# Order of TensorE's products with stationary weight columns: blocks of eight and eight in place of two and two

## The chip, the cores and the metric

The kernel runs on one core of one Trainium2 chip. The metric is the device time of one execution in microseconds (us), smaller is better. Engines are called as in the profile: PE is TensorE (PEld its weight loads), ACT is ScalarE, DVE is VectorE, POOL is GpSimd, SP is SyncE.

## The reference

A decoder trunk of four layers over 256 tokens and 2048 features, in float32. Layers 0 and 3 use latent attention, layer 1 sparse attention, layer 2 sliding-window attention. Each layer is one block:

```python
h = rmsnorm(x, norm_in[i])
self_out, mq, gate = mixer(h, ...)             # one projection makes q/k/v or latents, mq and gate
mem_out = memory_attention(mq, mem_n @ w_mem_kv[i])
y = concatenate([self_out, mem_out], -1) * silu(gate)
x = x + y @ w_out[i]
```

and a last rmsnorm ends it. Most of the work is products of 256 rows with weight matrices that come from HBM (511.62 MB are moved in all).

## The kernel before

**Two parts for each number.** The products keep nearly float32 accuracy with operands of type fp32r. Each operand is split into a high part, its rounded copy, and a low part, what is left. `split` (L67 to L69) makes the high part on ACT (`copy_act`, L60) and the low part on DVE as a subtraction (L69). A product is then high × high + high × low + low × high.

**Two ways of multiplying.** `rows_by` (L240) holds feature columns stationary in PE and streams weights past them, up to 512 columns: three products for each half of the rows and each feature tile of 128 (L265, L266, L267). `columns_by` (L270), which is changed here, holds weight columns stationary and streams the features, so its result stands transposed. It makes 256 output columns in two halves j of 128. For each feature tile kt of 128 and each half it has

- one product of 512 columns (L285): the high weight part `wh` stationary, and streaming past it both parts of the features, 256 columns each, side by side; the accumulator `acc[j]` keeps the two results apart in one PSUM bank,
- one product of 256 columns (L289): the low weight part `wl` stationary, and the high features streaming; it is added to the first half of `acc[j]`.

Each product has a weight load of its own (128 × 128). The order written in the code is, for each feature tile: two products of 512 (j = 0, 1), then two of 256 (j = 0, 1). Four feature tiles make a block: one weight load from HBM by `stage` (L217, issued by SP into one of five `wr` buffers of 512 KB), one call of `other_work`, and two calls of `parts_of`, each of which splits the weights of two feature tiles, a `wh` and a `wl` of 128 × 512. There are three buffers for `wh` and three for `wl`.

`columns_by` serves the keys of the memory (`mk`, L432), the gates (`g`, L462), the memory queries (`mq`, L548) and, in the latent layers, the compressed queries (`cq`, L641), the queries (`qn`, L688) and the keys (`kn`, L693). It has 16, 12 or 4 feature tiles, always whole blocks. The results are combined by `total` (ACT and DVE) or by `head_parts`.

**What sets the order.** The program is written as straight code, and a scheduler of the framework gives each engine a fixed order, from the order of the code, a simulated timeline and the free buffers. Products of attention (L487 transposes, L565 and L586 memory attention, L719, L921, L924 scores, L455 transposes) get places among the projections. At run time each engine goes through its own order and waits at semaphores. Only a few instructions, mostly DMAs, are pinned to the order of the code.

Of the kernel before, what the change touches and what calls it, by code (L numbers as in the profile page):

```python
# [15 lines left out]
P = 128  # L16
S = 256
# [14 lines left out]
def kernel(ctx: ExitStack, tc: tile.TileContext, a: dict, out: bass.AP,  # L32
                             kinds=(0, 1, 2, 0)):
    nc = tc.nc
# [32 lines left out]
    def split(hi, lo, src):  # L67
        copy_act(hi, src)
        nc.vector.tensor_sub(lo, src, f32(hi))  # L69
# [136 lines left out]
    def stage(w, k0, m, cols, each=None):  # L206

        n = cols[1] if len(cols) == 2 else cols[1] * cols[4]
        wr = wp.tile([P, ST * 512], F32, name="wr", tag="wr", bufs=WR)
        src = w[k0 * P:(k0 + m) * P, :].rearrange("(k p) n -> p k n", p=P)  # L210
        dst = wr[:, :m * n].rearrange("p (k n) -> p k n", k=m)
        if each is not None:
            for k in range(m):
                tc.keep_in_program_order(nc.sync.dma_start(dst[:, k, :], src[:, k, cols[0]:cols[0] + n]))
                each(k0 + k)
        elif len(cols) == 2:
            nc.sync.dma_start(dst, src[:, :, cols[0]:cols[0] + n])  # L217
        else:
            c0, r, step, off, width = cols
            for k in range(m):  # L220
                nc.sync.dma_start(dst[:, k, :].rearrange("p (r c) -> p r c", r=r),
                                  src[:, k, c0:c0 + r * step].rearrange("p (r c) -> p r c", r=r)
                                  [:, :, off:off + width])
        return wr, n
# [4 lines left out]
    def other_work():  # L229
        for _ in range(2):  # L230
            if steps and next(steps[0], None) is None:
                steps.pop(0)

    def parts_of(wr, c0, n):
        wh = wp.tile([P, 512], F32R, name="wh", tag="wh", bufs=3)
        wl = wp.tile([P, 512], F32R, name="wl", tag="wl", bufs=3)
        split(wh[:, :n], wl[:, :n], wr[:, c0:c0 + n])
        return wh, wl
# [31 lines left out]
    def columns_by(xt, kts, w, k0, cols, name):  # L270

        acc = [ps.tile([P, 2, S], F32, name=f"acc_{name}{j}", tag="acc", bufs=4) for j in range(2)]
        for s in range(0, kts, 2 * ST):
            m = min(2 * ST, kts - s)
            wr, n = stage(w, k0 + s, m, cols)
            other_work()
            for k2 in range(0, m, 2):
                wh, wl = parts_of(wr, k2 * S, 2 * S)
                for k in range(2):
                    kt = s + k2 + k  # L280
                    q = xt[kt // 4]

                    for j in range(2):
                        o = k * S + j * P
                        nc.tensor.matmul(acc[j], wh[:, o:o + P], q[:, :, kt % 4, :],  # L285
                                         start=kt == 0, stop=False)
                    for j in range(2):
                        o = k * S + j * P
                        nc.tensor.matmul(acc[j][:, 0, :], wl[:, o:o + P], q[:, 0, kt % 4, :],  # L289
                                         start=False, stop=kt == kts - 1)  # L290
        return acc

    def total(acc, name="z"):
# [70 lines left out]
    def memory():  # L364
# [54 lines left out]
        for i in range(depth):  # L419
            w = a["w_mem_kv"][i]  # L420
            for p_ in range(2):
                begins = i == p_ == 0
                if begins:

                    pinned.append(0)
                    acc = rows_by(mT, 16, w, 0, (MEMW, 512), "mv", prepare, each)
                    pinned.pop()
                    mrow = [memory_rows(c) for c in range(4)]
                else:
                    values(i, p_, rows_by(mT, 16, w, 0, (MEMW + p_ * 512, 512), "mv"))  # L430
                for h in (2 * p_, 2 * p_ + 1):
                    acck = columns_by(mT, 16, w, 0, (h * 256, 256), "mk")  # L432
                    if begins and h == 0:
                        row_scales(mrow)
                        values(i, p_, acc)
                    keys(i, h, acck)
                step = 2 * i + p_
                if begins:

                    not_before(f32(mT[3])[:, 0, 3, :1])  # L440
                    late_constants()
                    bias_table(0)
                    bias_table(1)
                if 1 <= step < 5:
                    steps.append(nm.first_chunk(step - 1))
# [13 lines left out]
    def gate(nm, w, c0):  # L459
        gT = act.tile([P, 4, S], F32, name="gT", tag="gT", bufs=2)  # L460
        for h in range(2):
            acc = columns_by(nm.at, 16, w, 0, (c0 + h * S, S), "g")  # L462
            for j in range(2):
                z = total(acc[j])
                hz = wk.tile([P, S], F32, name="hz", tag="z", bufs=3)
                nc.vector.tensor_mul(hz, z, nm.half)
                th = wk.tile([P, S], F32, name="th", tag="e", bufs=4)
                nc.scalar.activation(th, hz, AF.Tanh)
                nc.vector.scalar_tensor_tensor(gT[:, 2 * h + j, :], th, 1.0, hz, op0=OP.add, op1=OP.mult)
        return gT  # L470
# [65 lines left out]
    def memory_project(nm, i, w, mq0, g0, part, behind):  # L536
        kT, qT = [], []
        if part == 0:
            not_before(behind)
        v = [act.tile([P, 2, 512], F32R, name="mvr", tag="aux", bufs=AUX) for z in range(2)]  # L540
        pin = tc.keep_in_program_order if part == 0 else lambda inst: inst
        for z in range(2):
            pin(nc.gpsimd.dma_start(v[z], mv[i][part][:, z]))
        for h in range(2):
            k = act.tile([P, 2, 2, S], F32R, name="mkr", tag="pq", bufs=PQ)
            pin(nc.gpsimd.dma_start(k, mkT[i][2 * part + h]))
            kT.append(k)
            acc = columns_by(nm.at, 16, w, 0, (mq0 + part * 512 + h * 256, 256), "mq")  # L548
            q = act.tile([P, 2, 2, S], F32R, name="mqT", tag="pq", bufs=PQ)
            head_parts(q, acc)  # L550
            qT.append(q)
        return nm, kT, v, qT, gate(nm, w, g0 + 2048 + part * 512)
# [538 lines left out]
```

## Time and profile before

| | |
|---|---|
| median of 3 runs | 2592.52 us (2592.51 to 2592.64) |
| the profiled execution | 2594.19 us |
| its span, first to last instruction | 2592.4 us |
| mean granted TensorE clock | 0.998 |
| ACT waiting for PE's products of L285 with `acc_g`, before `wh` | 175.5 us in 254 waits |

The profile is of one execution. A row of the groups gives line, engine, operation, output <- inputs, shape and count, then the busy time in us and the mean ns of one, then the idle time of the engine just before. In the timeline a row gives the start in us, the length in us, engine, line, operation and count; neighbours of one kind are merged to one row, which runs from the start of the first to the end of the last. Products overlap: one starts while the one before it still drains, so the distance between starts is shorter than the length of one. A row of the waits says who waited for whom, the total in us, how often, and the longest.

### The profile page before, as it was taken

Reading aid. Unit: us, or ns where it says so; the run is one execution under the profiler, and the core shown is the slowest. Engines: PE = TensorE matmul, PEld = TensorE weight load, DVE = VectorE, ACT = ScalarE, POOL = GpSimd, SP = SyncE. Lnnn points to the kernel's source line nnn. Section 1 sums busy time; section 2 is a strip of 40 time slices with the busy share of each in tenths; the row PEclk is TensorE's granted clock in tenths of the full one; section 3 lists DMA queues with packets and bytes.
Section 4 is the critical chain, followed back from the end, with each engine's and each line's share of the span. In section 5 each row is a group of like instructions: output and inputs, shape, how many; then the busy total and the mean of one; then the engine's idle time right before and its main releaser. Section 6 shows DMA issues by size and latency. Waiting matters only on the chain.

```text
span 2592.4 us, 41637 instructions
## 1 busy us (share of the span) xinstructions
PE 2574.6 (99%) x14038; PEld 2213.6 (85%) x14038; DVE 1875.6 (72%) x4126; ACT 1619.6 (62%) x3435; POOL 67.3 (3%) x123
## 2 busy tenths in 40 slices
PE   9999999999999999999999999999999999999998
PEld 7888898888888888888888888888889888888886
DVE  6666667667776686877778776777778767676667
ACT  6555556556656566667666666676666655665655
POOL 1000000000000010000000000000000000000000
PEclk9999999999999999999999999999999999999999
DMA  9887777666676667566556575555655766566764
GB/s 302 255 256 257 242 214 234 184 171 190 193 202 201 199 215 249 165 202 191 184 170 197 170 226 168 176 172 184 195 157 152 231 185 166 170 168 182 212 178 132
DMA packets 456279, 511.62 MB, mean 197 GB/s; under 512 B 68944, under 2 KB 351840, under 8 KB 454912
## 3 DMA queue, kind: packets, MB, share of 16 engines
q1 hardware_dynamic: 442544, 451.68, 58.3%
q0 software_dynamic: 13088, 56.16, 6.8%
q8 instruction: 110, 1.80, 0.3%
q10 hardware_dynamic: 432, 1.11, 0.1%
q14 instruction: 105, 0.86, 0.1%
HBM read 489.91 MB, written 31.56 MB: 201 GB/s over the span
## 4 chain that ended last, share of the span: by engine, by line
PE 91%; DVE 0%; ACT 0%; issue 0%; ACTq 0%
PE acc_g L285 14%; PE acc_g L289 7%; PE acc_wo L265 7%; PE acc_wo L266 7%; PE acc_wo L267 7%; PE acc_mq L285 5%; PE acc_cq L285 3%; PE acc_qn L285 3%; PE acc_mq L289 2%; PE acc_mk L285 2%; PE acc_q L266 2%; PE acc_q L267 2%; PE acc_q L265 2%; PE acc_cq L289 2%; PE acc_qn L289 2%; PE ptp L487 1%
## 5 line engine op out<-in xcount | busy, mean ns | idle before, releaser
L69 DVE TENSOR_TENSOR wl<-wr,wh 128x512 fp32r<-128x512 f32 (+2 forms) x1728 | 1165.2, 677 | 630.1 <-ACT wh L60 609.4
L60 ACT ACTIVATE wh<-wr 128x512 fp32r<-128x512 f32 (+2 forms) x1728 | 1070.0, 621 | 806.9 <-PE acc_g L285 175.5
L285 PE MATMUL acc_g<-xT,wh 128*128 128x512 f32 x1536 | 486.6, 396 | 0.0
L289 PEld LDWEIGHTS acc_g<-xT,wl 128*128 128x128 f32 x1536 | 284.5, 188 | 60.4
L289 PE MATMUL acc_g<-xT,wl 128*128 128x256 f32 x1536 | 310.2, 280 | 0.0
L266 PE MATMUL acc_wo<-wl,y 128*128 128x512 f32 x768 | 303.4, 395 | 0.2 <-DVE wl L69 0.2
L267 PE MATMUL acc_wo<-wh,y 128*128 128x512 f32 x768 | 298.0, 390 | 0.0
L285 PEld LDWEIGHTS acc_g<-xT,wh 128*128 128x128 f32 x1536 | 238.4, 189 | 4.5
L265 PE MATMUL acc_wo<-wh,y 128*128 128x512 f32 x768 | 240.3, 392 | 0.1
L266 PEld LDWEIGHTS acc_wo<-wl,y 128*128 128x128 f32 x768 | 144.3, 188 | 28.4 <-DVE wl L69 0.6
L267 PEld LDWEIGHTS acc_wo<-wh,y 128*128 128x128 f32 x768 | 144.3, 188 | 27.8
L265 PEld LDWEIGHTS acc_wo<-wh,y 128*128 128x128 f32 x768 | 142.3, 188 | 29.2 <-ACT y L60 1.0
L285 PE MATMUL acc_mq<-xT,wh 128*128 128x512 f32 x512 | 161.6, 396 | 0.0
L285 PE MATMUL acc_mk<-mT,wh 128*128 128x512 f32 x512 | 161.5, 396 | 0.0
L978 DVE TENSOR_TENSOR x<-x,acc_wo 128x512 f32<-128x512 f32 x192 | 126.1, 681 | 5.7 <-PE acc_wo L267 5.6
L285 PE MATMUL acc_qn<-cT,wh 128*128 128x512 f32 x384 | 121.2, 397 | 0.0
L285 PE MATMUL acc_cq<-xT,wh 128*128 128x512 f32 x384 | 120.9, 396 | 0.0
L289 PEld LDWEIGHTS acc_mk<-mT,wl 128*128 128x128 f32 x512 | 96.1, 188 | 22.8 <-DVE wl L69 0.4
L289 PEld LDWEIGHTS acc_mq<-xT,wl 128*128 128x128 f32 x512 | 93.9, 188 | 20.1
L289 PE MATMUL acc_mq<-xT,wl 128*128 128x256 f32 x512 | 103.1, 282 | 0.0
L266 PE MATMUL acc_q<-wl,xT 128*128 128x512 f32 x256 | 101.2, 395 | 0.0
L289 PE MATMUL acc_mk<-mT,wl 128*128 128x256 f32 x512 | 101.1, 278 | 0.0
(307 smaller groups left out, 4264.8 us busy)
## 6 DMA issues: line engine op xcount, KB each, us to landing
wr<-in_w_out_dram SPq DMA_DIRECT2D x192, 512.0 KB, 3.6
wr<-in_w_in_a_dram SPq DMA_DIRECT2D x176, 512.0 KB, 3.9
wr<-in_w_mem_kv_dram SPq DMA_DIRECT2D x120, 512.0 KB, 4.7
wr<-in_w_in_b_dram SPq DMA_DIRECT2D x112, 512.0 KB, 3.5
wr<-in_w_in_c_dram SPq DMA_DIRECT2D x104, 512.0 KB, 3.5
wr<-in_w_uq_dram SPq DMA_DIRECT2D x192, 128.0 KB, 2.7
wr<-in_w_uq_dram SPq DMA_DIRECT2D x48, 256.0 KB, 3.7
tab<-flat POOLq DMA_DIRECT2D x8, 1536.0 KB, 9.3
```

What stands on the lines that cost most here:

```text
L60: inst = nc.scalar.activation(o, i, AF.Copy, scale=scale)
L69: nc.vector.tensor_sub(lo, src, f32(hi))
L265: nc.tensor.matmul(acc[t][:, :n], xh, wh[:, :n], start=first, stop=False)
L266: nc.tensor.matmul(acc[t][:, :n], xh, wl[:, :n], start=False, stop=False)
L267: nc.tensor.matmul(acc[t][:, :n], xl, wh[:, :n], start=False, stop=last)
L285: nc.tensor.matmul(acc[j], wh[:, o:o + P], q[:, :, kt % 4, :], start=kt == 0, stop=False)
L289: nc.tensor.matmul(acc[j][:, 0, :], wl[:, o:o + P], q[:, 0, kt % 4, :], start=False, stop=kt == kts - 1)
L487: nc.tensor.transpose(tp[:, i * P:(i + 1) * P], es[b][:, k * P:(k + 1) * P], ident)
L978: nc.vector.tensor_add(xs, xs, acc[t])
```

## The change

`columns_by` gathers the products with `wl` of a block in a list and issues them after the block's products with `wh`. A block is then eight products of 512 columns (feature tile by feature tile, j = 0, 1), and after them eight of 256 in the same order. The splits are still made two feature tiles at a time, in the place of the first product that needs them. Operands, shapes, counts, buffers and the sums stay the same, except for the order in which the terms are added.

```diff
-            for k2 in range(0, m, 2):
-                wh, wl = parts_of(wr, k2 * S, 2 * S)
-                for k in range(2):
-                    kt = s + k2 + k
-                    q = xt[kt // 4]
-
-                    for j in range(2):
-                        o = k * S + j * P
-                        nc.tensor.matmul(acc[j], wh[:, o:o + P], q[:, :, kt % 4, :],
-                                         start=kt == 0, stop=False)
-                    for j in range(2):
-                        o = k * S + j * P
-                        nc.tensor.matmul(acc[j][:, 0, :], wl[:, o:o + P], q[:, 0, kt % 4, :],
-                                         start=False, stop=kt == kts - 1)
+
+            rest = []
+            for k in range(m):
+                if k % 2 == 0:
+                    wh, wl = parts_of(wr, k * S, 2 * S)
+                kt = s + k
+                q = xt[kt // 4]
+                for j in range(2):
+                    o = k % 2 * S + j * P
+                    nc.tensor.matmul(acc[j], wh[:, o:o + P], q[:, :, kt % 4, :],
+                                     start=kt == 0, stop=False)
+                    rest.append((acc[j][:, 0, :], wl[:, o:o + P], q[:, 0, kt % 4, :], kt == kts - 1))
+            for o, l, r, last in rest:
+                nc.tensor.matmul(o, l, r, start=False, stop=last)
```

## The prediction

> **What bounds the kernel now.** I read the page first, then the waits of PE, then PE's timeline where these products run undisturbed.
>
> ```profile
> span 2592.4 us, 41637 instructions
> PE 2574.6 (99%) x14038; PEld 2213.6 (85%) x14038; DVE 1875.6 (72%) x4126; ACT 1619.6 (62%) x3435; POOL 67.3 (3%) x123
> ...
> PE 91%; DVE 0%; ACT 0%; issue 0%; ACTq 0%
> ```
> ```profile
> PE acc_mv L265 <- ACT wh L60: 3.2, 4, 1.1
> PE wu L102 <- DVE ones L98: 1.1, 1, 1.1
> PE o L950 <- DVE pT L69: 0.3, 1, 0.3
> PE acc_wo L266 <- DVE wl L69: 0.2, 1, 0.2
> ```
>
> PE is busy for 99% of the span, carries 91% of the chain that ended last, and in all waited 4.8 us for another engine, never at the changed lines. So the end is set by how fast PE goes through its products. A busy time of 99% says nothing of that speed, since the ends of overlapping products are modelled; the distance from one start to the next does. The products in question:
>
> ```profile
> L285 PE MATMUL acc_g<-xT,wh 128*128 128x512 f32 x1536 | 486.6, 396 | 0.0
> L289 PE MATMUL acc_g<-xT,wl 128*128 128x256 f32 x1536 | 310.2, 280 | 0.0
> L285 PE MATMUL acc_mq<-xT,wh 128*128 128x512 f32 x512 | 161.6, 396 | 0.0
> L285 PE MATMUL acc_mk<-mT,wh 128*128 128x512 f32 x512 | 161.5, 396 | 0.0
> L285 PE MATMUL acc_qn<-cT,wh 128*128 128x512 f32 x384 | 121.2, 397 | 0.0
> L285 PE MATMUL acc_cq<-xT,wh 128*128 128x512 f32 x384 | 120.9, 396 | 0.0
> ...
> L285 PE MATMUL acc_kn<-cT,wh 128*128 128x512 f32 x128 | 42.5, 400 | 0.0
> ```
>
> L285 has 1536 + 512 + 512 + 384 + 384 + 128 = 3456 products of 512 columns, and by the code L289 has as many of 256. A block (four feature tiles) holds eight of each, so there are 3456 / 8 = **432 blocks**. The means of 396 and 280 ns are latencies; the pace comes from a stretch of the timeline in which nothing else is in PE's stream (columns: start, length of the merged group, count):
>
> ```profile
> 120.81 0.62 PE L285 MATMUL acc_mk<-mT,wh 128*128 128x512 f32 x2
> 121.26 0.40 PE L289 MATMUL acc_mk<-mT,wl 128*128 128x256 f32 x2
> ...
> 142.39 0.63 PE L285 MATMUL acc_mk<-mT,wh 128*128 128x512 f32 x2
> 142.86 0.39 PE L289 MATMUL acc_mk<-mT,wl 128*128 128x256 f32 x2
> 143.09 0.40 PE L265 MATMUL acc_mv<-wh,mT 128*128 128x512 f32 x1
> ```
>
> From 120.81 to 143.09 lie the 128 products of two calls, eight blocks: 22.28 / 8 = **2.785 us a block**, 0.696 for each group of two wide and two narrow ones. Of that the two wide take 142.86 − 142.39 = 0.47 and the two narrow 143.09 − 142.86 = 0.23, so 0.233 and 0.115 each.
>
> **The change, part by part.** Counts of products, weight loads, splits, DMAs and bytes stay as they are; only PE's order changes, from two and two to eight and eight. What must be priced is the start-to-start distance inside long runs. The trace has pieces of such runs: one stretch where the scheduler joined the groups to three or more wide and four narrow, and long runs of 256-column products of other lines, each with a weight load of its own.
>
> ```profile
> 566.35 0.86 PE L285 MATMUL acc_g<-xT,wh 128*128 128x512 f32 x3
> 567.05 0.39 PE L289 MATMUL acc_g<-xT,wl 128*128 128x256 f32 x2
> 567.27 0.62 PE L285 MATMUL acc_g<-xT,wh 128*128 128x512 f32 x2
> 567.74 0.64 PE L289 MATMUL acc_g<-xT,wl 128*128 128x256 f32 x4
> 568.21 0.63 PE L285 MATMUL acc_g<-xT,wh 128*128 128x512 f32 x2
> ```
> ```profile
> 1459.28 1.59 PE L565 MATMUL msp<-mkr,mqT 128*128 128x256 f32 x12
> 1460.70 1.48 PE L586 MATMUL mo<-pT,mvr 128*128 128x256 f32 x11
> ```
>
> *Narrow products.* A group of n with length T has n − 1 distances, T less the latency of the last. For L565 that is (1.59 − 0.28) / 11 = 0.119, for L586 (1.48 − 0.28) / 10 = 0.120, for the four of L289 (0.64 − 0.28) / 3 = 0.120. In pairs they cost 0.115. So a narrow product deep in a run costs some 4 to 5 ns more. The first after a wide one keeps its place: the pair's 0.39 to 0.40 less 0.28 is 0.11 to 0.12. For a block I take 0.114 + 7 × 0.1195 = 0.951 against 8 × 0.115 = 0.920: +31 ns. Bounds: 7 × 0.118 at the best (four in 568.21 − 567.74 = 0.47 us), 7 × 0.1205 at the worst, so +20 to +38.
>
> *Wide products.* The three at 566.35 give (0.86 − 0.396) / 2 = 0.232; up to the first narrow one, (567.05 − 566.35) / 3 = 0.233. In pairs it was 0.233. The third digit is at the edge of what the rows show, so I take 0.2315 for a wide product in a run, 8 × 0.0015 = −12 ns a block, between −16 (0.231) and +4 (0.2335).
>
> *Sum.* +31 − 12 = +19 ns a block, 432 blocks: **+8.2 us**. The bounds are +4 and +42 ns, +1.7 and +18 us.
>
> A rule speaks for no change at all: by the Trainium skill (TensorE: Matmul & The Clock Gate, "LDWEIGHTS (loading the stationary operand)" and "Back-to-back issue gap") loading 128 columns takes 128 / 1.2 = 107 ns and a stream of 256 columns 256 / 2.4 + 2.5 = 109 ns, so that a load hides behind either kind of product and the order costs nothing; by it the sum would be 0. The 119 to 120 ns in the long runs above are longer than both figures, so the trace doesn't bear it out.
>
> *Waits and buffers.* The order on PE also sets when the split weights are needed and freed. Three tiles each of wh and wl rotate; ACT makes wh, DVE makes wl.
>
> ```profile
> L69 DVE TENSOR_TENSOR wl<-wr,wh 128x512 fp32r<-128x512 f32 (+2 forms) x1728 | 1165.2, 677 | 630.1 <-ACT wh L60 609.4
> L60 ACT ACTIVATE wh<-wr 128x512 fp32r<-128x512 f32 (+2 forms) x1728 | 1070.0, 621 | 806.9 <-PE acc_g L285 175.5
> ```
> ```profile
> DVE wl L69 <- PE acc_g L285: 2.6, 4, 0.7
> DVE wl L69 <- DMA wr<-in_w_in_a_dram: 2.1, 3, 0.7
> ```
>
> The first narrow product of a block comes 8 × 0.2315 = 1.85 us in, instead of 0.47, so a late wl is better covered at a call's start; PE waits nothing there now, so that gains nothing. For the tiles in between: before, wl's slot was free two pairs (2 × 1.39) and 0.47 us ahead of its use, 3.25 us. Now both wl tiles of a block are held to its end. One slot is free a whole block and 1.85 us ahead, 4.6 us; the other only when half of the narrow products are through, 0.47 + 1.85 + 0.47 = 2.8 us ahead. The subtraction takes 0.677, and its wh, whose slot is freed among the wide products, is done before. So 2.1 us are left for what stands ahead of it in DVE's queue. A new thing is that DVE, which stood for PE in the row above in four places, will stand at such a wl more often; behind it in its queue are the sums, softmax steps and residual additions that PE needs later, and SP's weight loads, whose buffers the wl subtraction frees. With DVE busy for 72% I take nothing for it, and a tail (below).
>
> Products of other lines stand in PE's stream as before, but the scheduler may set them at other places. Such a place costs some 0.07 us: the wide product just after a group of transposes begins a row of four, whose length is
>
> ```profile
> 566.05 1.16 PE L285 MATMUL acc_g<-xT,wh 128*128 128x512 f32 x4
> ```
>
> so that its first distance is 1.16 − 0.86 = 0.30 instead of 0.23. Fifty places more or fewer would be ±3.5 us. I take none.
>
> The profiled execution took 2594.19 us, 1.8 outside its span; 2594.19 + 8.2 = 2602.4. It lies 1.67 above the median of the runs, 2592.52, which makes my forecast **2600.7 us**.
>
> **The rivals.**
>
> *Each change of width costs (faster).* In some places the scheduler broke the pairs to single products:
>
> ```profile
> 1200.99 0.40 PE L285 MATMUL acc_g<-xT,wh 128*128 128x512 f32 x1
> 1201.22 0.28 PE L289 MATMUL acc_g<-xT,wl 128*128 128x256 f32 x1
> ...
> 1203.82 0.40 PE L285 MATMUL acc_g<-xT,wh 128*128 128x512 f32 x1
> ```
>
> Eight wide and eight narrow take 2.83 us here, 45 ns more than in pairs, with 16 changes of width instead of 8: 5.6 ns a change. If that were the rule, the six changes taken out of a block would save 34 ns, 432 times: 14.6 us, 2578 us. It decides if a narrow product behind a narrow one starts within 7x + 0.114 + 8 × 0.2315 = 2.785, x = 0.117 us. For it speaks this stretch; against it the four at 567.74 and the eleven-fold rows, all over 0.117.
>
> *No change.* Either each weight load hides behind the product ahead of it, whichever its width, so that 0.233 and 0.115 hold in any order (2592.5 us); or the scheduler breaks up the runs again, as it made singles at 1200.99 and a four at 567.74; or wide and narrow balance (0.231 and 0.1185). All leave 2592 to 2597 us. The first is what the rule of the Trainium skill named above would give. For it: the two terms have opposite signs and a few ns each. Against: almost all of the old stream stands in the order of the code.
>
> *A late wl (slower by more).* If the 2.1 us aren't enough, PE stands at the second half of the narrow products. One subtraction, 0.677 us, in one block of ten is 43 × 0.677 = 29 us on top of 8: 2630 us. Against it: 3.25 us were enough everywhere, and DVE has 28% of its time free.
>
> **How the numbers follow.** A measurement of this kernel can tell about 0.2%, 5.2 us, from no change. The forecast has 0.58, and since its lower bound is +1.7, 0.06 of that lies within 5.2 us; no change 0.22; a cost of each change 0.10; a late wl 0.10. So faster 0.10, same 0.28, slower 0.62. The forecast's own range is 2594 to 2611; places moved by the scheduler and a few late wl widen it to 2590 to 2615, which leaves out most of the faster case and half of the late one.
>
> **What would show it.** In the timeline of the new kernel, undisturbed rows of L285 with x8 and of L289 with x8: their length less 0.396 or 0.28, over seven, should be 0.231 to 0.233 and 0.118 to 0.120, and a call of sixteen feature tiles should take 4 × 2.804 = 11.2 us instead of 11.14. PE's waits should stay near 5 us. I am wrong if the narrow rows run at 0.117 or less, if rows of x8 are rare, or if DVE's wl appears among PE's waits.

## The result and the profile after

The changed kernel takes **2604.92 us** (median of 6 runs, 2603.89 to 2607.07), the kernel before 2592.82 us in the 6 runs then at hand. The ratio is **1.0046, 95% interval 1.0036 to 1.0057**: 12.1 us slower, between 9.3 and 14.8. The forecast was 8.2 us. The two profiled executions, 2603.98 and 2594.19 us, lie 9.8 us apart; that of before stands 1.4 us above its median and that of after 0.9 below, which is the rest.

The page of the changed kernel (L286 holds the wide products now, L290 the narrow ones):

```profile
span 2602.2 us, 41634 instructions
PE 2581.4 (99%) x14038; PEld 2224.3 (85%) x14038; DVE 1860.6 (72%) x4126; ACT 1617.7 (62%) x3435; POOL 66.7 (3%) x123
...
PE 89%; DVE 1%; ACT 0%; issue 0%; ACTq 0%; DVEq 0%
...
L286 PE MATMUL acc_g<-xT,wh 128*128 128x512 f32 x1536 | 397.6, 394 | 0.0
...
L290 PE MATMUL acc_g<-xT,wl 128*128 128x256 f32 x1536 | 226.7, 283 | 0.0
```

PE is still the bound and has the same products. In the rows of the gates (`acc_g`) the busy time of the wide products fell from 486.6 to 397.6 us, that of the narrow ones from 310.2 to 226.7, in a kernel that became slower. This is a trap: the busy time of a group is the time in which at least one of it is under way, and neighbours of one group overlap more in longer runs. The means, 394 and 283 ns (396 and 280 before), hardly moved. Only distances between starts show the pace. Here they are for PE in an undisturbed stretch of the timeline:

```profile
130.13 2.00 PE L286 MATMUL acc_mk<-mT,wh 128*128 128x512 f32 x8
131.98 0.64 PE L290 MATMUL acc_mk<-mT,wl 128*128 128x256 f32 x4
132.45 1.09 PE L286 MATMUL acc_mk<-mT,wh 128*128 128x512 f32 x4
133.38 0.63 PE L290 MATMUL acc_mk<-mT,wl 128*128 128x256 f32 x4
133.85 1.09 PE L286 MATMUL acc_mk<-mT,wh 128*128 128x512 f32 x4
134.78 1.12 PE L290 MATMUL acc_mk<-mT,wl 128*128 128x256 f32 x8
135.74 2.00 PE L286 MATMUL acc_mk<-mT,wh 128*128 128x512 f32 x8
137.58 1.11 PE L290 MATMUL acc_mk<-mT,wl 128*128 128x256 f32 x8
138.53 2.00 PE L286 MATMUL acc_mk<-mT,wh 128*128 128x512 f32 x8
140.37 1.11 PE L290 MATMUL acc_mk<-mT,wl 128*128 128x256 f32 x8
141.32 2.00 PE L286 MATMUL acc_mk<-mT,wh 128*128 128x512 f32 x8
```

Two whole blocks run from 135.74 to 141.32, 2.79 us each (2.785 before). The eight wide ones take 137.58 − 135.74 = 1.84, the narrow ones 0.95. Not all blocks are whole: from 130.13 to 135.74 the scheduler broke two blocks to 8, 4, 4, 4, 4, 8, and they take 2.805 us each. Over the whole trace 262 runs of narrow products are eight long and 280 four long.

The waits, first of PE, then the longest of DVE's:

```profile
PE acc_mv L265 <- ACT wh L60: 3.4, 4, 1.3
PE wu L102 <- DVE ones L98: 1.1, 1, 1.1
PE acc_wo L265 <- ACT wh L60: 1.1, 1, 1.1
PE acc_wo L266 <- DVE wl L69: 1.0, 2, 0.7
PE acc_wo L265 <- DVE z L296: 0.7, 1, 0.7
```
```profile
DVE wl L69 <- ACT wh L60: 287.9, 490, 3.9
DVE wl L69 <- PE acc_g L290: 134.4, 153, 2.0
DVE wl L69 <- PE acc_mk L290: 59.1, 58, 2.0
DVE wl L69 <- PE acc_cq L290: 36.8, 32, 1.5
DVE wl L69 <- PE acc_mq L290: 36.2, 41, 2.0
DVE wl L69 <- PE acc_qn L290: 23.0, 22, 1.6
```

DVE stands some 290 us at `wl` until narrow products free a tile. Before, it stood there 4.7 us, for PE's wide products. PE itself waits 7 to 8 us instead of 4.8, and now also for late operands of the products with `w_out`.

**Where the 9.8 us are.** For each of PE's products I took the distance to the next start, put it down to the product that begins it, and summed by kind over the whole trace of each profiled execution. The counts of each kind are the same in both kernels. With what lies ahead of the first product (1.1 us) and behind the start of the last (13.3 in both), the sums make up the span.

| distances begun by | number | before, us | after, us | difference |
|---|---|---|---|---|
| the first 30 products | 30 | 9.0 | 9.9 | +0.9 |
| wide products (512 columns) | 3456 | 809.6 | 801.3 | −8.3 |
| narrow products (256 columns) | 3456 | 406.2 | 414.9 | +8.8 |
| products in row order (`rows_by`) | 5139 | 1131.3 | 1138.8 | +7.5 |
| all others | 1956 | 222.0 | 222.9 | +0.9 |

So the changed products cost almost nothing together: what the wide ones gain, the narrow ones lose, and +0.5 us is left. The loss lies with products whose order in the code nobody touched. Those in row order take 7.5 us more, and nearly all of it, 7.3 us, is in distances of over 0.3 us, of which there are 123 instead of 102. Of the 7.5 us, 4.8 are at the products with `w_out`, 2.1 in the memory stage (`acc_mv`) and 0.6 at `acc_q`. The profile of the run contig below, which has the old order, shows what differs without any change of order: 0.8 us in the first 30 products, 0.9 in `acc_mv`, and under 0.1 in each of the other rows.

One sum that looks natural misleads here. The distances from one changed product to another changed one are 6664 before and 6667 after, and they grew by 5.6 us, from 1172.2 to 1177.8. But after the change 45 more of them are begun by a wide product and 42 fewer by a narrow one, because other products now break in at other places. At 0.234 and 0.118 us each that alone is 5.6 us. It is no loss of pace. The "stream +4 to +6 us" in some expectations below comes from this sum.

### The profile page after: what moved, and what is told of

Same layout as the page of the kernel before. It is cut to its first block, busy times and chain, and to the rows that moved or that the text cites. A ratio compares the mean times of both kernels' runs of the same rounds, so it can differ in the third digit from the quotient of the medians.

```text
span 2602.2 us, 41634 instructions
## 1 busy us (share of the span) xinstructions
PE 2581.4 (99%) x14038; PEld 2224.3 (85%) x14038; DVE 1860.6 (72%) x4126; ACT 1617.7 (62%) x3435; POOL 66.7 (3%) x123
## 3 DMA queue, kind: packets, MB, share of 16 engines
q10 hardware_dynamic: 432, 1.11, 0.1%
## 4 chain that ended last, share of the span: by engine, by line
PE 89%; DVE 1%; ACT 0%; issue 0%; ACTq 0%; DVEq 0%
PE acc_g L286 14%; PE acc_g L290 7%; PE acc_wo L265 7%; PE acc_wo L266 7%; PE acc_wo L267 7%; PE acc_mq L286 5%; PE acc_cq L286 3%; PE acc_qn L286 3%; PE acc_mq L290 2%; PE acc_q L266 2%; PE acc_q L267 2%; PE acc_q L265 2%; PE acc_cq L290 2%; PE acc_qn L290 2%; PE acc_mk L286 2%; PE ptp L487 1%
## 5 line engine op out<-in xcount | busy, mean ns | idle before, releaser
L286 PE MATMUL acc_g<-xT,wh 128*128 128x512 f32 x1536 | 397.6, 394 | 0.0
L286 PEld LDWEIGHTS acc_g<-xT,wh 128*128 128x128 f32 x1536 | 272.6, 189 | 45.2
L290 PEld LDWEIGHTS acc_g<-xT,wl 128*128 128x128 f32 x1536 | 216.7, 190 | 18.9
L290 PE MATMUL acc_g<-xT,wl 128*128 128x256 f32 x1536 | 226.7, 283 | 0.0
L286 PE MATMUL acc_mq<-xT,wh 128*128 128x512 f32 x512 | 132.9, 394 | 0.0
L286 PE MATMUL acc_mk<-mT,wh 128*128 128x512 f32 x512 | 129.8, 393 | 0.0
L286 PEld LDWEIGHTS acc_mk<-mT,wh 128*128 128x128 f32 x512 | 91.9, 189 | 17.3 <-issue 0.6
L286 PEld LDWEIGHTS acc_mq<-xT,wh 128*128 128x128 f32 x512 | 90.6, 189 | 15.1
L266 PE MATMUL acc_mv<-wl,mT 128*128 128x512 f32 x256 | 101.1, 395 | 0.0
L267 PE MATMUL acc_mv<-wh,mT 128*128 128x512 f32 x256 | 100.3, 392 | 0.0
L267 PE MATMUL acc_q<-wh,xT 128*128 128x512 f32 x256 | 100.3, 392 | 0.0
L286 PE MATMUL acc_qn<-cT,wh 128*128 128x512 f32 x384 | 99.7, 394 | 0.0
```

The lines of the kernel that those rows point to most:

```text
L266: nc.tensor.matmul(acc[t][:, :n], xh, wl[:, :n], start=False, stop=False)
L267: nc.tensor.matmul(acc[t][:, :n], xl, wh[:, :n], start=False, stop=last)
L290: nc.tensor.matmul(o, l, r, start=False, stop=last)
```

## The experiments

The theory at that time: long runs cost pace, and `wl` tiles held to a block's end make splits late for the products that follow. Rival A: the held tiles are the whole cost. Rival B: each change of width costs 5.6 ns, so that longer runs gain. Rival C: the pace is the whole cost. Each time stands beside runs of the kernel before on the same chip (2592.6 to 2593.6 us).

**Runs of four, no tile held over.**

```diff
-                for k in range(2):
+                for low in range(2):
+                    for k in range(2):
...
+                        for j in range(2):
+                            o = k * S + j * P
+                            if low:
+                                nc.tensor.matmul(acc[j][:, 0, :], wl[:, o:o + P], q[:, 0, kt % 4, :], ...)
+                            else:
+                                nc.tensor.matmul(acc[j], wh[:, o:o + P], q[:, :, kt % 4, :], ...)
```

> Four wide, then four narrow products, for each pair of feature tiles, so each wl is freed as soon as in the kernel before and no wl is held over. My theory (pace in long runs costs a little, the rest of the 12 us is late splits): the changed kernel's own stretches of four and four took 1.401 us for eight products, so a block takes 2.80 us instead of 2.785, 432 blocks, +6.5 us, and no new waits: 2599 us. Rival A (holding wl is the whole cost): same as before, 2593 us. Rival B (each change of width costs 5.6 ns): four changes fewer a block, -10 us, 2583 us.

Measured: 2600.42 us, ratio 1.0028 (1.0017 to 1.0039), +7.3 us. PE's timeline:

```profile
84.22 1.09 PE L289 MATMUL acc_mk<-mT,wh 128*128 128x512 f32 x4
85.14 0.64 PE L286 MATMUL acc_mk<-mT,wl 128*128 128x256 f32 x4
...
96.82 1.08 PE L289 MATMUL acc_mk<-mT,wh 128*128 128x512 f32 x4
```

From 84.22 to 96.82 there are nine groups of four and four: 1.400 us each, 2.80 a block, as expected. Over the whole trace the wide products take 4.3 us less than before and the narrow ones 9.3 more, so 5.0 of the 5.7 us between the two profiled executions are pace. Rival B falls, since half of the changes of width are gone and it is slower, not faster. Rival A isn't decided by this run: rows of four cost pace, but the rows of eight of the changed kernel cost only 0.5 us in sum.

**Single products in turn.**

```diff
                     for j in range(2):
                         o = k * S + j * P
                         nc.tensor.matmul(acc[j], wh[:, o:o + P], q[:, :, kt % 4, :],
                                          start=kt == 0, stop=False)
-                    for j in range(2):
-                        o = k * S + j * P
                         nc.tensor.matmul(acc[j][:, 0, :], wl[:, o:o + P], q[:, 0, kt % 4, :],
                                          start=False, stop=kt == kts - 1)
```

> One wide, one narrow product in turn, for every feature tile and half, buffers used as in the kernel before. My theory (the pace depends on the neighbours): 0.353 us a pair as in the stretch at 1201 us of the kernel before, 2.83 us a block instead of 2.785, +19 us: 2612 us. Rival A (holding wl is the whole cost): 2593 us. Rival B (each change of width costs 5.6 ns) gives the same 2612 as mine here; the two part at runs of four and eight.

Measured: 2604.77 us, ratio 1.0044 (1.0030 to 1.0057), +11.6 us.

```profile
527.17 0.40 PE L285 MATMUL acc_qn<-cT,wh 128*128 128x512 f32 x1
527.40 0.28 PE L287 MATMUL acc_qn<-cT,wl 128*128 128x256 f32 x1
...
529.99 0.40 PE L285 MATMUL acc_qn<-cT,wh 128*128 128x512 f32 x1
```

Eight pairs take 2.82 us, as expected. But only 1829 of the 3456 narrow products stand alone; the scheduler put nearly all others together in twos. Of +19 us that leaves some 10, and the changed products do take 8.7 us more. The size was missed because I had counted on the written order, not on the scheduled one. Another 4.1 us lie in the memory stage (`acc_mv`), some of them in a stretch of 3.4 us in which the granted clock was 0.50, and 1.0 at the products with `w_out`, although no tile is held longer here.

**The two feature parts side by side in SBUF.**

```diff
-            q = act.tile([P, 2, 4, S], F32R, name="xT", tag="xT", bufs=4)
+            q = act.tile([P, 4, 2, S], F32R, name="xT", tag="xT", bufs=4).rearrange("p k v c -> p v k c")
```

(the same for `mT` and `cT`; order of the kernel before)

> Order of the kernel before, but the two parts of a feature tile lie side by side in SBUF, so that a wide product streams one stretch of 512 columns instead of two of 256 that lie 4 KB apart. In the kernel before such a wide product costs 0.233 us in pairs, and products of 512 columns in one stretch (L265 to L267) some 0.227. If the two stretches are the reason: up to 6 ns for 3456 products, -20 us, 2573 us. If it is the neighbourhood of narrow products, as the wide products late in a run of eight (0.227 us in two stretches) suggest, no change: 2593 us. I expect no change.

Measured: 2592.83 us, ratio 0.9998 (0.9989 to 1.0006). No change: the wide products sum to 809.5 us, against 809.6 before. What makes a wide product 0.233 us long in pairs isn't that it streams two stretches.

**Narrow products cut to 128 columns.**

```diff
-                    rest.append((acc[j][:, 0, :], wl[:, o:o + P], q[:, 0, kt % 4, :], kt == kts - 1))
+                    rest.append((acc[j][:, 0, :P], wl[:, o:o + P], q[:, 0, kt % 4, :P], kt == kts - 1))
```

> The changed kernel's order, with the narrow products cut to 128 of their 256 columns (the low weight part is left out for half of the rows). If a narrow product's pace in a run, 0.120 us, is its stream plus a fixed cost (wide ones late in a run: 0.227 us, so 0.107 less for 256 columns less), it falls to 0.067 us and the kernel by up to 3456 x 0.053 = 183 us. If it is the weight load that sets 0.120, it stays at 0.11 to 0.12 and the kernel loses less than 35 us. I lean to the first, but expect the load to be met on the way, near 0.108, the pace of the 128-column transposes: about -40 us.

Measured: one run of 2581.33 us, 23.6 less than the changed kernel.

```profile
84.99 0.56 PE L290 MATMUL acc_mk<-mT,wl 128*128 128x128 f32 x4
...
87.73 1.00 PE L290 MATMUL acc_mk<-mT,wl 128*128 128x128 f32 x8
88.57 2.08 PE L286 MATMUL acc_mk<-mT,wh 128*128 128x512 f32 x8
```

Four more products make a row (1.00 − 0.56) / 4 = 0.11 us a piece longer, although half of their columns are gone; in the changed kernel it was (1.11 − 0.64) / 4 = 0.118. So inside a row these products do not come closer than 0.11 us, and the 256-column product lies only 8 ns above that. It holds inside a row only: the eight narrow ones take 88.57 − 87.73 = 0.84 us, which leaves 0.06 for the first of them after seven at 0.112. The wide ones behind them got slower too (2.08 against 2.00 for eight). Over the whole trace the narrow products take 56.2 us less than in the changed kernel and the wide ones 25.4 more.

That the weight load sets the 0.11 is likely but not shown. The Trainium skill (TensorE: Matmul & The Clock Gate, "LDWEIGHTS (loading the stationary operand)") gives P / 1.2 ns for a load of P columns, by estimate 107 ns for these 128, and the 0.11 inside the rows agrees with it. It isn't a floor for every product with a load of its own, as this row of four transposes of 128 columns in the kernel before shows:

```profile
742.93 0.45 PE L455 MATMUL tr<-identr,qrs 128*128 128x128 f32 x4
743.22 1.16 PE L285 MATMUL acc_g<-xT,wh 128*128 128x512 f32 x4
```

They take (743.22 − 742.93) / 4 = 0.07 us each, with a load of 128 columns each.

**Tile counts.** Five `wl` tiles only fit with one buffer less for loaded weights, so there is a control for each order.

```diff
-PQ, AUX, WR, PT, WARM = 5, 4, 5, 4, 9
+PQ, AUX, WR, PT, WARM = 5, 4, 4, 4, 9
```

> Control for the next two: the kernel before with four instead of five buffers for the loaded weights, which makes room in SBUF. Neither theory says much; the load of the next block has 8 us instead of 11 us, so I expect 2593 to 2600 us, with most of any loss in the memory stage, where the DMA queues are busiest.

> The changed kernel with four weight buffers: both theories expect the distance to the control before_wr4 to be that of the change, +12 us (10 to 15).

Measured: 2595.18 us (ratio 1.0009, 1.0000 to 1.0018) with the old order, 2608.29 us (1.0059, 1.0046 to 1.0071) with the new one. The control costs 2.6 us, the change 13.1 us on top, as without it.

```diff
-        wl = wp.tile([P, 512], F32R, name="wl", tag="wl", bufs=3)
+        wl = wp.tile([P, 512], F32R, name="wl", tag="wl", bufs=5)
```

> The changed kernel with four weight buffers and five wl tiles instead of three, so that no wl waits for the narrow products of its own block. My theory (stream +4 to +6 us, late splits in the products that follow +6 us): the waits of DVE's wl for the narrow products (290 us) go, the stretches of PE are all eight and eight, and the distance to before_wr4 falls from +12 to +4 to +7 us. Rival A (holding wl is the whole cost): it falls to 0. Rival C (the pace alone): it stays at +12.

Measured: 2603.77 us, ratio 1.0046 (1.0033 to 1.0058), 8.6 us above the control. DVE's waits:

```profile
DVE wl L69 <- ACT wh L60: 600.8, 993, 4.6
DVE u L505 <- PE sp L921: 21.9, 29, 1.2
```

The waits for the narrow products are gone, 360 narrow runs are whole now, and the median falls by 4.5 us. The step goes the way of the theory, though the ranges of the two kernels' runs overlap. Rival A's 0 isn't reached, and 8.6 is more than the 4 to 7 expected. The sums by kind say more. At the products with `w_out` the control of the new order takes 5.0 us more than that of the old one, with five tiles 2.2. The changed products take 1.4 us more with three tiles and 0.2 with five, so rival C, the pace alone, falls. The rest is in the memory stage (`acc_mv` +5.8 us) and at `acc_iq` (+1.2). But this profiled execution is the longest of the five (2608.67 us), with two stretches of 3.4 us in the memory stage in which the granted clock was 0.50; the median of five has no profile.

**A short lead in the old order.** `bufs=2` for `wl`, the rest as before.

> The kernel before with two wl tiles instead of three: the cost of a short lead by itself, in the old order. A slot comes free 1.39 + 0.47 = 1.86 us ahead of its use, of which the subtraction takes 0.68. My theory: DVE's waits for PE rise to hundreds of us as in the changed kernel, and a part of them reaches PE as late splits: +5 to +20 us. If such waits cost PE nothing, so that the changed kernel's 12 us are pace alone: same as before.

Measured: 2613.89 us, ratio 1.0081 (1.0068 to 1.0095), +21.3 us. DVE's waits:

```profile
DVE wl L69 <- PE acc_g L289: 150.4, 205, 1.5
DVE wl L69 <- PE acc_mk L289: 64.0, 88, 1.2
DVE wl L69 <- PE acc_mv L266: 35.9, 55, 0.7
```

A lead of 1.86 us is too short, and DVE stands for PE as in the changed kernel. Here 15.8 of the 19.9 us between the profiled executions lie at the changed products themselves, which the changed kernel does not show, and 3.3 at those with `w_out`. The scheduler's order changed too, so that not all of it need be the lead. It was just above the 5 to 20 us that I expected.

**Four tiles of both parts.** `bufs=4` for `wh` and `wl`, four weight buffers.

> Order of the kernel before, four weight buffers, and four tiles each of wh and wl instead of three: a longer lead for both parts in the old order, 4.6 us for wl instead of 3.25. Two tiles cost 21 us. If the lead of three was enough (late splits reach PE there only in a few places): no change against before_wr4, 2595 us (2592 to 2597). If lead were the scarce thing in the kernel before too, some of its 13 us of long distances ahead of products in the row order would go: 2588 us. I expect the first.

> The changed order with four weight buffers and four tiles each of wh and wl. A wl no longer waits for the narrow products of its own block, and wh has one tile more. My theory (stream +4 to +6 us, the rest from late splits): DVE's waits for the narrow products go, and the distance to before_wr4, 13 us with three tiles and 9 us with five wl, is 4 to 9 us. If late splits come from the scheduler's new order of ACT and DVE and not from the tiles, it stays at 9 to 13 us. If holding wl were all: 0.

Measured: 2622.97 us (ratio 1.0112, 1.0097 to 1.0127) and 2621.86 us (1.0112, 1.0096 to 1.0129). Both expectations failed: with more tiles both kernels are 28 to 29 us slower than the kernel before, 26 to 27 us beyond the 2.6 of the control with three tiles in the old order. PE's waits in the old order:

```profile
PE o L950 <- DVE pT L69: 8.9, 3, 3.3
PE ptp L487 <- ACT e L60: 4.2, 3, 2.9
PE acc_wo L265 <- ACT y L60: 1.6, 1, 1.6
```

The loss in the old order is not at the changed products, which take the same time as in the control within 0.1 us. Distances begun by the products of attention and the other small ones grew by 17.4 us and those begun by products with `w_out` by 10.4; attention's weights (`e`, `pT`) come late from ACT and DVE. Part of it is a slower PE. After the wait of 3.00 us for `pT` the profile has

```profile
1219.55 1.86 PE L950 MATMUL o<-pT,vz 128*128 128x512 f32 x5 [3.00 <-DVE pT L69]
1221.22 0.63 PE L265 MATMUL acc_wo<-wh,y 128*128 128x512 f32 x1
1221.64 0.63 PE L266 MATMUL acc_wo<-wl,y 128*128 128x512 f32 x1
```

with starts 0.42 apart instead of 0.23, and the granted clock from 1218.70 to 1225.50 was 0.50. Three more stretches of 3.4 us are like it. By an estimate from these numbers that is some 7 of the 26 us in this execution; its mean clock is 0.995, against 0.998 in the control. With free tiles the scheduler can put splits earlier in the queues of ACT and DVE, ahead of the softmax; that this is what it did is only argued. As a yardstick for the change this pair is useless in its total. The pace inside it is not: the changed products take 1216.1 us in the old order and 1216.4 in the new.

## Why the prediction was right

Direction and range held, but the number came near by luck. The 8.2 us were forecast for the pace of the changed products, which cost 0.5 us; the 12 us that came are mostly longer gaps at other products, which the forecast put at nothing.

- **What bounds the kernel** was right: PE's stream, in which every us of the difference can be found.
- **Narrow products, +31 ns a block**: right in an undisturbed block, somewhat too big in all. Eight take 140.37 to 141.32 = 0.95 us, against 8 × 0.115 = 0.92. Over the trace they take 8.8 us more, where 432 × 31 ns would be 13.4.
- **Wide products, −12 ns**: this term was mis-sized. Eight take 1.84 us, against 1.864 in pairs: −24 ns. The row of eight, 2.00, less the row of four, 1.09, gives 0.2275 for each of the last four; the rows of before had at most four, and those run at 0.232 to 0.233. Over the trace they take 8.3 us less, where 432 × 12 ns would be 5.2. So the two terms cancel.
- **432 whole blocks**: only partly so, with 262 narrow runs of eight and 280 of four. In the stretches above whole blocks cost +5 ns and broken ones +20. That the sum over all is still only 0.5 us, 1 ns a block, must come from places where other products break in; which of them, I did not follow.
- **Waits, taken at nothing**: this was the step that failed. The products in row order lose 7.5 us. The table of PE's waits grew by only some 3 us, so that for more than half of that it names no cause. That DVE would stand at `wl` more often, as the prediction says, did come. So did one of its signs of being wrong: `wl` is among PE's waits, with 1.0 us (0.2 before). Four distances at the products with `w_out` are 0.6 to 1.2 us too long, together 3.5 of the 4.8 us there; before has none there that is over 0.35 us too long. In the profile two of the four wait for `wl`, one for `wh` and one for the sum `z` (L296) on DVE. The one for `wh`, in the timeline of ACT and PE:

```profile
1447.06 0.71 PE L265 MATMUL acc_wo<-wh,y 128*128 128x512 f32 x2
...
1447.61 0.63 PE L290 MATMUL acc_g<-xT,wl 128*128 128x256 f32 x4
...
1450.13 0.51 ACT L512 ACTIVATE e<-u,mn 128x256 f32<-128x256 f32 x1 [0.23 <-DVE mn L507]
...
1450.64 0.40 ACT L468 ACTIVATE th<-hz 128x256 f32<-128x256 f32 x1
1450.94 0.61 ACT L60 ACTIVATE wh<-wr 128x512 fp32r<-128x512 f32 x1
...
1451.61 0.50 PE L265 MATMUL acc_wo<-wh,y 128*128 128x512 f32 x1 [1.05 <-ACT wh L60]
```

  The last four narrow products of a gate stand behind the first products with `w_out`. The `wh` that PE needs next stands behind a softmax and a tanh in ACT's queue, and PE loses 1.2 us. These four places are the same with four weight buffers and are gone with five `wl` tiles, where one of 0.6 us stands elsewhere. That fits the held tiles as a cause, but the place shown is a matter of ACT's order, and the tile count changes that order too.
- **No change**: its third form, that wide and narrow balance, is what the changed products did, at 0.230 and 0.119 us in rows of eight. The 109 ns of the rule from the Trainium skill that the prediction cites did not come: a narrow product in a run costs 0.118 to 0.120 us.
- **The other rivals**: that each change of width costs was refuted by runs of four. A late `wl` that holds PE up in its own block did not come, since PE's waits name no L290; the longer gaps at the products with `w_out`, of which late splits are a part, cost some 5 us, not 29.

What stays open: how much of the late splits is the held tile and how much the scheduler's other order. Five tiles take away 2.8 of the 5.0 us at `w_out`, but each change of a tile count also changed the order of ACT and DVE, and one such change came with 26 us. The 2.1 us in the memory stage and the 0.9 at the start are little more than what differs between two profiles of the old order. In the memory stage single waits of 0.3 to 2 us ahead of the products of `acc_mv` change place from kernel to kernel, and nothing here separates them.

## What to carry to other kernels

Price a new order of products by the distance between starts, in runs like those that it will make; busy times of groups can fall while the kernel slows. When you sum distances, put each down to the product that begins it, so that both kernels have the same counts. Long runs of one width win nothing here: 2.4 ns less for a wide product, 2.5 ns more for a narrow one. What such an order does to the splits and to the products that follow is part of its price: here that was more than the pace. With two `wl` tiles the old order lost 21 us, and more tiles moved other work.

## What was not expected of the hardware

- The pace of a 512-column product depends on what ran before it: 0.233 us in pairs with narrow ones, 0.2275 as the fifth to eighth of a run, with the same operands. It isn't the layout of the streamed operand (no change with one stretch). By an estimate from these numbers an endless run would take 8 × (0.2275 + 0.120) = 2.78 us a block, 5 ns or 0.2% less than pairs: by order alone there is next to nothing to win.
- Halving the columns of the narrow products, 3456 × 128 columns, took only 23.6 us off the kernel, 7 ns for each: in a row they still start 0.11 us apart. Transposes of 128 columns, with loads of their own too, start 0.07 apart.
- In some executions the granted clock fell to 0.50 for 3.4 us, or 6.8 in one case, and the products of that stretch started 0.42 us apart instead of 0.23. With four tiles of both parts it happened four times in one execution, the first time during a wait of PE of 3.00 us.
